# A two-layer decoder trunk on one core: the last norm's sums made on all partitions by products with ones, and its power taken on 128x256 values

## The chip, the cores and the metric

The kernel runs on one core of a Trainium2 chip. The metric is the device time of one execution in microseconds (us). The core has five engines that run side by side, each through its own instructions in order: TensorE (PE in the profile, its weight loads PEld), VectorE (DVE), ScalarE (ACT), GpSimd (POOL) and SyncE (SP), which here only issues DMA transfers. They wait for each other by semaphores. TensorE's results go into PSUM, which the kernel uses as eight banks of 128 partitions by 512 float32; the other operands lie in SBUF, as tiles of 128 partitions too.

## The reference

The reference is a trunk of two decoder layers for 256 tokens with 2048 channels. Layer 0 mixes the tokens by multi-scale retention with 8 heads, layer 1 by a short gated convolution; each is followed by a SwiGLU feed-forward of width 5632. Each sub-layer begins with an RMS norm with a scale and a shift made from a conditioning vector, its output is multiplied by a gate, and it is added to `x`. What matters here is the last step, one more RMS norm over the 2048 channels of each token with a gain for each channel:

```python
def rms_norm(x, gain=None):
    xf = x.astype(jnp.float32)
    y = xf * lax.rsqrt(jnp.mean(xf * xf, axis=-1, keepdims=True) + EPS)
    if gain is not None:
        y = y * gain.astype(jnp.float32)
    return y
...
    return rms_norm(x, final_g).astype(x.dtype)
```

## The kernel before

**Layout.** `x` lies in SBUF with channels on partitions and tokens along the row: 16 tiles `x[j]` of 128 channels by 256 tokens, in float32. A sum over the channels of a token is therefore a sum over 16 tiles and over 128 partitions.

**The bulk of the work.** The weights come from memory as blocks of 128 rows by 2048 columns (`raw`, line 290, issued by SP). Each half of a block is parted into a high part (`hi`, ScalarE, line 295) and a low part (`lo`, VectorE, line 296). For each 128 x 128 piece of weights TensorE makes three products, high with high, high with low and low with high, in `product` (lines 338 and 341) and `packed` (lines 361 to 363). The order of TensorE's instructions is that of the program (`manual_schedule`, line 188); the other engines' instructions are put in order by a scheduler with priorities.

**The last output of layer 1.** `swiglu` (line 743) ends in `output` (line 500) with `last` set. For each of the 16 column tiles, VectorE adds gate times product to `x[j]` (lines 518 and 519, for the last tile line 511, called by way of `packed` so that one instruction does). Then ScalarE squares it and VectorE adds the square to `acc` (`squares`, lines 387 and 388). The last tile's square goes into a tile of its own, `acc1` (line 512, recorded as line 384), so the norm's sum is that of two tiles, `acc = [acc, acc1]`. `with_gain` (line 792) has ScalarE multiply each new `x[j]` by the final gain into one of nine output parts (line 796).

**The last norm.** `rstd` (line 419) makes 1/sqrt(mean + eps) in three steps, each a helper that the other norms use too.

- `norm_sums` (line 391): for each half of the tokens, a product with the tile `acc` as weights and a single column of ones as the moving operand, one for each of the two tiles. Its result has one token on each partition: 128 x 2 values in PSUM (line 396).
- `norm_roots` (line 402): VectorE multiplies by 1/2048 and adds eps on 128 x 2 values (line 405); GpSimd raises them to the power -0.5 (line 407, `half` holds -0.5). What GpSimd reads and writes here lies in SBUF.
- `norm_spread` (line 410): two products, whose weights are a column of roots broadcast to 128 columns and whose moving operand is the identity matrix (line 414). Every partition then has all 256 roots in PSUM.

The result `rb` lies in PSUM. ScalarE copies it into `rbs` in SBUF (line 806). The 16 tiles of the output are multiplied by the roots, 11 of them on VectorE with `rb` from PSUM (line 810) and 5 on GpSimd with `rbs` (line 812), as `OUT_SPLIT` deals them out. When a part of one to three tiles is done, SP writes it to memory (line 813), in the order of the nine parts.

The float32 products of lines 396 and 414 leave two matmul records each in the trace; the products of the bulk leave one each.

Of the kernel before, what the change touches and what calls it, by code (L numbers as in the profile page):

```python
# [53 lines left out]


class Group:
    """Output columns of a matrix that are worked out together, in the order of their rows."""

    def __init__(self, cols, width=P, ks=range(KT)):
        self.cols, self.width, self.ks = cols, width, list(ks)  # L60


def ret_in_groups():
    """The first heads' queries, keys and gates are made of two spans of rows, the first of them ahead."""
    early, late = range(FIRST_KS), range(FIRST_KS, KT)
    ahead, heads = [], []
    for h in range(HEADS):
        q = [Q0 + h * DK + i * P for i in range(2)]
        k = [K0 + h * DK + i * P for i in range(2)]
        g = [G0 + h * DV + i * P for i in range(4)]  # L70
        v = Group([V0 + h * DV], DV)
        if h < EARLY_HEADS:
            ahead.append([q, k, g[:2], g[2:]])
            qkg = [Group(c, ks=late) for c in ahead[-1]]
        else:
            qkg = [Group(c) for c in (q, k, g[:2], g[2:])]
        heads.append((qkg, v))
    first = Group([c for pairs in ahead[:2] for pair in pairs for c in pair], ks=early)
    second = [[Group(c, ks=early) for c in pairs] for pairs in ahead[2:]]
    return first, second, heads  # L80
# [4 lines left out]


def out_groups(rows, parts, tail, lead):
    """The first columns' products with the last rows, which are made last, come after the others."""
    n = rows // P // parts
    cols = [c * P for c in range(KT)]  # L90
    out = []
    for s in range(parts):
        ks = range(s * n, (s + 1) * n)
        led = cols[:lead]
        out.append([Group(led, ks=ks[:-tail])] + [Group([c], ks=ks[-tail:]) for c in led])
        out[-1] += [Group([c], ks=ks) for c in cols[lead:]]
    return out
# [18 lines left out]


def in_use_order():
    """Each group of the weights, with its matrix and the matrix's index, in the order of use."""
    yield "ret_w_in", 0, RET_FIRST  # L120
    for groups in RET_SECOND:
        for g in groups:
            yield "ret_w_in", 0, g
    for h, (qkg, v) in enumerate(RET_HEADS):
        for g in qkg[:2] + [v] + qkg[2:]:
            yield "ret_w_in", 0, g
        if h % (HEADS // 2) == HEADS // 2 - 1:
            for g in RET_OUT[h // (HEADS // 2)]:
                yield "ret_w_out", 0, g
    for layer in range(DEPTH):  # L130
        if layer == 1:
            for g in CONV_IN:
                yield "conv_w_in", 0, g
            for g in CONV_OUT:
                yield "conv_w_out", 0, g
        for part in range(2):
            for g in FFN_IN[part]:
                yield "ffn_w_in", layer, g
            for g in FFN_OUT[part]:
                yield "ffn_w_out", layer, g  # L140


def laid_out(arrays):
    """The weights in the order of their use, as blocks of 128 rows and CHUNK columns."""
    total = sum(len(g.cols) * g.width * len(g.ks) for _, _, g in in_use_order())
    out = np.empty((total // CHUNK, P, CHUNK), np.float32)
    at = 0
    for key, i, g in in_use_order():
        for k in g.ks:
            for c in g.cols:  # L150
                o = at % CHUNK
                out[at // CHUNK, :, o : o + g.width] = arrays[key][i, k * P : (k + 1) * P, c : c + g.width]
                at += g.width
    assert at == total and total % CHUNK == 0
    return out
# [16 lines left out]
def trunk(ctx: ExitStack, tc: tile.TileContext, x_in, c_in, pos_in, w_mod, cols_in, tab_in, w_all, out):  # L172
# [14 lines left out]

    ctx.enter_context(tc.manual_schedule(engines={mybir.EngineType.PE}))

# [1 line left out]
    ones = const.tile([P, P], F32, tag="ones", name="ones")  # L191
    nc.vector.memset(ones, 1.0)
    cb = const.tile([P, D], F32, tag="cb", name="cb")
# [30 lines left out]
    half = const.tile([P, 2], F32, tag="half", name="half")  # L224
    nc.vector.memset(half, -0.5)

# [1 line left out]
    mod_a = [[const.tile([P, KT], F32, tag=f"a{l}{i}", name=f"a{l}{i}") for i in range(2)] for l in range(DEPTH)]  # L228
    mod_s = [[const.tile([P, KT], F32, tag=f"s{l}{i}", name=f"s{l}{i}") for i in range(2)] for l in range(DEPTH)]
    mod_g = [[const.tile([P, KT], F32, tag=f"g{l}{i}", name=f"g{l}{i}") for i in range(2)] for l in range(DEPTH)]  # L230
# [27 lines left out]
    units, allowed = [0], [0.0]  # L258

    def paced(n):  # L260
        """Counts n more products of 128 x 128 weights, and works out the modulations due by now."""
        units[0] += n
        due = 0
        for (a, i), (b, j) in zip(plan_mod, plan_mod[1:]):
            if units[0] >= a:
                due = min(j, i + (units[0] - a) * (j - i) // (b - a))
        allowed[0] = min(allowed[0] + n * MOST, 2.0) if n <= 64 else 0.0
        while todo and n_mod - len(todo) < due and allowed[0] >= 1.0:
            allowed[0] -= 1.0
            modulation(*todo.pop())  # L270
# [2 lines left out]
        while any(m[:2] == (layer, which) and m[2] <= last for m in todo):  # L273
            modulation(*todo.pop())

# [1 line left out]
    order = [(g, k, c) for _, _, g in in_use_order() for k in g.ks for c in g.cols]  # L277
    order.reverse()
    n_halves = w_all.shape[0] * CHUNK // HALF
# [19 lines left out]
    prepared = [0]  # L299

    def take(group, k, col):
        """The next weights' high and low parts."""
        assert order.pop() == (group, k, col)
        i = taken_cols[0] % HALF
        if i == 0:
            if ready and taken_cols[0]:
                ready.pop(0)
            while len(ready) < 1 + AHEAD * (units[0] >= early):
                n = len(ready)
                prepare()  # L310
                if len(ready) == n:
                    break
        taken_cols[0] += group.width
        return [t[:, i : i + group.width] for t in ready[0]]
# [4 lines left out]
    asides, since = [], [0]  # L319

    def ticked(n):
        """Between products, the next step of what runs beside them."""
        since[0] += n
        if asides and since[0] >= asides[0][0]:
            asides.pop(0)[1]()
            since[0] = 0

    def product(g, act, base=0, before=None, banks=None, last=True):
        """Banks [columns, (high product, the rest), tokens], one for each of the group's columns."""
        fresh = not banks  # L330
        banks = banks or [bank() for _ in g.cols]
        for k in g.ks:
# [13 lines left out]
        return banks  # L346

    def packed(g, act, base=0, before=None, between=None, banks=None):
        """Banks [columns, two of the group's columns, tokens]."""
        banks = banks or [bank() for _ in g.cols[::2]]  # L350
        for k in g.ks:
            if before:
# [20 lines left out]
        return dst  # L373

    def split(dst, src, at=slice(0, S)):
        """dst [128, (high, low), tokens] of src."""
        nc.scalar.copy(dst[:, 0, at], src)
        nc.vector.tensor_tensor(dst[:, 1, at], src, dst[:, 0, at].bitcast(F32), op=ALU.subtract)  # L378

# [1 line left out]
    def squares(acc, t, tag="acc"):  # L381
        if acc is None:
            acc = tmp(tag, bufs=1)
# [5 lines left out]
        return acc  # L389

    def norm_sums(accs):
        """The sums over partitions, a token to a partition."""
        pt = bank()
        for t in range(2):
            for i, acc in enumerate(accs):
# [4 lines left out]
        return pt  # L400

    def norm_roots(pt, n):
        """1 / sqrt(mean + eps)."""
        r = tmp("rs", (P, 2), bufs=4)
        nc.vector.tensor_scalar(r, pt[:, 0, 0:2], 1.0 / n, EPS, op0=ALU.mult, op1=ALU.add)
        r2 = tmp("rs", (P, 2), bufs=4)
# [1 line left out]
        return r2  # L408

    def norm_spread(r):  # L410
        """The roots on all partitions, in PSUM."""
        pb = bank()
        for t in range(2):
            nc.tensor.matmul(
# [27 lines left out]
    h = [h_all[:, j, :, :S] for j in range(KT)]  # L442

    def scaled_only(layer, norm, j):
        """h[j] without the norm and the shift."""
        needed(layer, SC2 if norm else SC1, j)
        a = mod_a[layer][norm][:, j : j + 1]
        nc.scalar.activation(h[j][:, 0, :], x[j], AF.Identity, scale=a)
# [2 lines left out]
        )  # L451

    def normed(accs, layer, norm, g):
        """
        The sums of the first columns, made from rows without the norm and the shift: the norm is a factor of
        each token, and the shift's product is one more token
        (twice, for these products take an even number of them). Beside them the roots, and then h, are made.
        """
        needed(layer, SH2 if norm else SH1)
        shift = mod_s[layer][norm].unsqueeze(2).to_broadcast([P, KT, 2])  # L460
        ends = [h_all[:, :, i, S:] for i in range(2)]
# [36 lines left out]
        return [lambda dst=None, pt=pt: total(pt, dst) for pt in banks]  # L498

    def output(groups, act, which, last, after=None):  # L500
        """x += gate * product; if last, tiles whose sums are those of the new x's squares."""
        layer, gate = which[0], mod_g[which[0]][which[1] == GT2]
        first, *groups = groups
        base, acc = first.ks[0], None
# [17 lines left out]
            if after:  # L522
                after(j)

# [1 line left out]
    with ExitStack() as inner:  # L526
        rm = inner.enter_context(tc.tile_pool(name="rmid", bufs=1))

# [139 lines left out]
            return both  # L668

        def mixed(head, both, v, sg):  # L670
            """The rest of a head, in steps."""
            accs, os, pts = [None], [], []

            def outputs(half):
# [27 lines left out]
            return list(zip(STEPS, [lambda: outputs(0), lambda: outputs(1), roots, ends]))  # L702

        def pair(head, i):
            """Two columns' sums [columns, two, tokens]."""
            g = RET_HEADS[head][0][i]
            (pt,) = packed(g, h)
            if (head, i) not in ahead:
# [54 lines left out]

    acc = swiglu(0, acc, lambda j: scaled_only(1, 0, j))

# [1 line left out]
    mid = [mpool.tile([P, 2, S], F32R, tag=f"mid{i}", name=name("mid")) for i in range(KT)]  # L767
    pending, done = [], 0
    for i, g in enumerate(CONV_IN):
# [29 lines left out]

    acc = swiglu(1, acc, with_gain)  # L800

# [1 line left out]
    assert not todo  # L803
    rb = rstd(acc, D)
    rbs = tmp("rbs", pool=mpool, bufs=1)
    nc.scalar.copy(rbs, rb)
    for (i, j, engine), o in zip(OUT_SPLIT, parts):
        for n in range(j - i):
            if engine == "vector":
# [39 lines left out]
```

## Time and profile before

| what | us |
|---|---|
| median of 3 runs | 2667.12 |
| lowest and highest run | 2664.53, 2668.72 |
| profiled execution, first to last instruction (its span) | 2660.6 |
| TensorE busy in it | 2621.9 (99%) |
| VectorE busy | 2017.8 (76%) |
| ScalarE busy | 1248.4 (47%) |
| GpSimd busy | 214.0 (8%) |
| mean granted TensorE clock | 0.998 of full speed |

The profile records one execution; its span is counted from its first instruction to its last, and no other time of that execution is given. The median of the runs is 6.5 us above that span. A row of a timeline gives the start in us from the span's start, the duration in us, the engine, the line of the kernel, the operation, the tiles written and read, the shapes and how many instructions were merged; in brackets the time that the engine sat idle before it, and who ended that idle time. A row on one line gives the count, the least, median and greatest duration in ns, and the first and last start in us.

### The profile page before, as it was taken

Reading aid. Unit: us, or ns where it says so; the run is one execution under the profiler, and the core shown is the slowest. Engines: PE = TensorE matmul, PEld = TensorE weight load, DVE = VectorE, ACT = ScalarE, POOL = GpSimd, SP = SyncE. Lnnn points to the kernel's source line nnn. Section 1 sums busy time; section 2 is a strip of 40 time slices with the busy share of each in tenths; the row PEclk is TensorE's granted clock in tenths of the full one; section 3 lists DMA queues with packets and bytes.
Section 4 is the critical chain, followed back from the end, with each engine's and each line's share of the span. In section 5 each row is a group of like instructions: output and inputs, shape, how many; then the busy total and the mean of one; then the engine's idle time right before and its main releaser. Section 6 shows DMA issues by size and latency. Waiting matters only on the chain.

```text
span 2660.6 us, 40134 instructions
## 1 busy us (share of the span) xinstructions
PE 2621.9 (99%) x16044; PEld 2335.6 (88%) x16044; DVE 2017.8 (76%) x2655; ACT 1248.4 (47%) x1782; POOL 214.0 (8%) x278
## 2 busy tenths in 40 slices
PE   6999999999999999999999999999999999999998
PEld 5898988999989888888888898888998888888887
DVE  8968988887698877777777889878887665555554
ACT  3444543444456444334444454444554443444443
POOL 4310000011000010100000001100000000000000
PEclk9999999999999999999999999999999999999999
DMA  9976667777677877777777768776777765555553
GB/s 374 400 265 242 251 217 296 267 270 263 250 267 261 312 281 267 298 271 284 285 268 282 268 219 321 287 282 256 268 269 256 264 220 190 185 185 189 189 190 127
DMA packets 96957, 687.69 MB, mean 258 GB/s; under 512 B 10753, under 2 KB 12545, under 8 KB 13825
## 3 DMA queue, kind: packets, MB, share of 16 engines
q1 hardware_dynamic: 96770, 685.13, 69.3%
q8 instruction: 125, 2.05, 0.3%
q14 instruction: 62, 0.51, 0.1%
HBM read 682.99 MB, written 2.10 MB: 257 GB/s over the span
## 4 chain that ended last, share of the span: by engine, by line
PE 76%; issue 19%; DVE 3%; DMA 0%; POOL 0%; ACT 0%; DVEq 0%; ACTq 0%; POOLq 0%
PE bank L338 35%; PE bank L341 18%; PE bank L363 4%; PE bank L361 4%; PE bank L362 4%; PE bank L634 2%; PE bank L635 2%; PE bank L636 2%; PE bank L477 1%; PE bank L476 1%; PE bank L478 1%; DVE raw L238 1%; DVE lo L296 1%; PE bank L680 0%; DMA raw<-w_mod 0%
## 5 line engine op out<-in xcount | busy, mean ns | idle before, releaser
L296 DVE TENSOR_TENSOR lo<-raw,hi 128x1024 fp32r<-128x1024 f32 x912 | 1113.5, 1223 | 561.1 <-ACT hi L295 559.2
L295 ACT CAST hi<-raw 128x1024 fp32r<-128x1024 f32 x912 | 953.9, 1050 | 1087.3 <-PE bank L338 638.5
L338 PE MATMUL bank<-h,hi 128*128 128x512 f32 x3296 | 1155.2, 395 | 0.0
L341 PE MATMUL bank<-h,lo 128*128 128x256 f32 x3296 | 925.5, 281 | 0.0
L338 PEld LDWEIGHTS bank<-h,hi 128*128 128x128 f32 x3296 | 622.7, 189 | 144.9
L338 PE MATMUL bank<-mid,hi 128*128 128x512 f32 x2100 | 731.1, 395 | 0.1
L341 PEld LDWEIGHTS bank<-h,lo 128*128 128x128 f32 x3296 | 623.3, 189 | 0.0
L341 PE MATMUL bank<-mid,lo 128*128 128x256 f32 x2100 | 583.8, 278 | 0.0
L338 PEld LDWEIGHTS bank<-mid,hi 128*128 128x128 f32 x2100 | 394.1, 188 | 92.2 <-DVE mid L378 0.4
L238 DVE SCALAR_TENSOR_TENSOR raw<-raw,cb 128x2048 f32<-128x2048 f32 x192 | 438.5, 2284 | 5.0 <-DMA raw<-w_mod 4.8
L341 PEld LDWEIGHTS bank<-mid,lo 128*128 128x128 f32 x2100 | 395.0, 188 | 0.0
L363 PE MATMUL bank<-h,lo 128*128 128x256 f32 x1024 | 292.4, 286 | 10.0 <-DVE lo L296 10.0
L361 PE MATMUL bank<-h,hi 128*128 128x256 f32 x1024 | 290.6, 284 | 2.8 <-ACT hi L295 2.8
L362 PE MATMUL bank<-h,hi 128*128 128x256 f32 x1024 | 290.3, 284 | 0.6 <-DVE h L432 0.5
L363 PEld LDWEIGHTS bank<-h,lo 128*128 128x128 f32 x1024 | 193.8, 189 | 14.4 <-DVE lo L296 14.4
L361 PEld LDWEIGHTS bank<-h,hi 128*128 128x128 f32 x1024 | 195.7, 191 | 3.5 <-ACT hi L295 3.3
L362 PEld LDWEIGHTS bank<-h,hi 128*128 128x128 f32 x1024 | 193.9, 189 | 2.3 <-DVE h L432 2.3
L243 POOL TENSOR_SCALAR mcol<-msum,cols 128x1 f32<-128x1 f32 x64 | 63.6, 994 | 549.6 <-DVE raw L238 549.6
L634 PE MATMUL bank<-hi,h 128*128 128x512 f32 x256 | 101.4, 396 | 0.0
L635 PE MATMUL bank<-lo,h 128*128 128x512 f32 x256 | 101.0, 395 | 0.0
L636 PE MATMUL bank<-hi,h 128*128 128x512 f32 x256 | 101.0, 394 | 0.0
L370 ACT COPY low<-bank 128x256 f32<-128x256 f32 x254 | 90.7, 364 | 11.7 <-PE bank L341 9.0
(122 smaller groups left out, 1811.6 us busy)
## 6 DMA issues: line engine op xcount, KB each, us to landing
raw<-w_all SPq DMA_DIRECT2D x456, 1024.0 KB, 4.9
raw<-w_mod SPq DMA_DIRECT2D x192, 1024.0 KB, 5.0
x<-x_in SPq DMA_DIRECT2D x4, 512.0 KB, 5.7
out<-out SPq DMA_DIRECT2D x5, 256.0 KB, 2.9
decay<-tab_in SPq DMA_DIRECT2D x8, 128.0 KB, 3.0
out<-out SPq DMA_DIRECT2D x3, 128.0 KB, 2.3
out<-out SPq DMA_DIRECT2D x1, 384.0 KB, 2.7
cols<-cols_in SPq DMA_DIRECT2D x1, 160.0 KB, 7.2
```

The costliest lines, as they stand in the source:

```text
L238: nc.vector.scalar_tensor_tensor(raw, raw, 1.0, cb, op0=ALU.mult, op1=ALU.mult, accum_out=total)
L295: nc.scalar.copy(hi, raw)
L296: nc.vector.tensor_tensor(lo, raw, hi.bitcast(F32), op=ALU.subtract)
L338: nc.tensor.matmul(pt, hi, h, start=fresh and k == g.ks[0], stop=False, skip_group_check=True)
L341: nc.tensor.matmul(pt[:, 1, :], lo, h[:, 0, :], start=False, stop=last and k == g.ks[-1], skip_group_check=True)
L361: nc.tensor.matmul(pt, hi, h[:, 0, :], start=first, stop=False, skip_group_check=True)
L362: nc.tensor.matmul(pt, hi, h[:, 1, :], start=False, stop=False, skip_group_check=True)
L363: nc.tensor.matmul(pt, lo, h[:, 0, :], start=False, stop=last, skip_group_check=True)
L370: nc.scalar.copy(low[:, at], pt[:, 1, at])
L634: nc.tensor.matmul(o, ht[:, 0, :], hi, start=k == 0, stop=False)
L635: nc.tensor.matmul(o, ht[:, 0, :], lo, start=False, stop=False)
L636: nc.tensor.matmul(o, ht[:, 1, :], hi, start=False, stop=k == KT - 1)
```

## The change

The three helpers are no longer called for the last norm; the other norms keep them. In their place:

- The whole tile of ones, 128 x 128, is the weights, and the two tiles `acc` (128 x 256) are the moving operands. The two products add up in one PSUM bank, and every partition gets the sums of all 256 tokens.
- VectorE makes the mean plus eps of 128 x 256 values, from PSUM into `mean` in SBUF.
- GpSimd takes the power of 128 x 256 values, from `mean` into `rbs` in SBUF.
- ScalarE copies `rbs` into a PSUM bank, which is the new `rb`.

The multiplications, their split between the engines and the writes stay as they are. The diff, without the comments and docstrings that it also takes out:

```diff
-    rb = rstd(acc, D)
+    pt = bank()[:, 0, :]
+    for i, t in enumerate(acc):
+        nc.tensor.matmul(pt, ones, t, start=i == 0, stop=i == len(acc) - 1)
+    mean = tmp("mean", pool=mpool, bufs=1)
+    nc.vector.tensor_scalar(mean, pt, 1.0 / D, EPS, op0=ALU.mult, op1=ALU.add)
     rbs = tmp("rbs", pool=mpool, bufs=1)
-    nc.scalar.copy(rbs, rb)
+    nc.gpsimd.tensor_tensor(rbs, mean, half[:, 0:1].to_broadcast([P, S]), op=ALU.pow)
+    rb = bank()[:, 0, :]
+    nc.scalar.copy(rb, rbs)
     for (i, j, engine), o in zip(OUT_SPLIT, parts):
```

## The prediction

> **What bounds the kernel now.** I read the page first, then the table of busy time by stage for the last 60 us, then the timeline of the last 20 us, and then the rows of single lines that price the new instructions.
>
> ```profile
> span 2660.6 us, 40134 instructions
> PE 2621.9 (99%) x16044; PEld 2335.6 (88%) x16044; DVE 2017.8 (76%) x2655; ACT 1248.4 (47%) x1782; POOL 214.0 (8%) x278
> ```
>
> ```profile
> 2600.00:2646.80 46.80, 46.80 (x292) 41.90 (x291) 24.62 (x32) 18.69 (x26) 0.00 (x0) 1.00 0.31 113
> 2646.80:2651.50 4.70, 2.33 (x14) 1.87 (x12) 0.65 (x2) 1.19 (x3) 0.69 (x1) 0.75 0.00 0
> 2651.50:2660.60 9.10, 0.00 (x0) 0.00 (x0) 3.73 (x11) 0.00 (x0) 3.46 (x5) 0.50 0.63 231
> ```
>
> The columns of the second table are the stretch and its length, the busy time and count of PE, PEld, DVE, ACT and POOL, then the granted clock, the DMA share and GB/s. The page says that TensorE bounds the kernel as a whole. That says nothing about this change, which lies behind the last weight product: up to 2646.8 TensorE is busy for 46.80 of 46.80 us, in the next 4.70 us for 2.33, and then never again. The last 14 us are a chain in which one engine at a time works and the others wait. Here is that chain:
>
> ```profile
> 2647.01 0.48 DVE L511 SCALAR_TENSOR_TENSOR x<-bank,g,x 128x256 f32<-128x256 f32 x1 [5.93 <-PE bank L363]
> 2647.52 0.42 ACT L384 ACTIVATE acc<-x 128x256 f32<-128x256 f32 x1 [6.50 <-DVE x L511]
> 2647.85 0.49 ACT L796 ACTIVATE out<-x,cols 128x256 f32<-128x256 f32 x1
> 2647.99 0.74 PEld L396 LDWEIGHTS bank<-ones,acc 128*128 128x128 f32 x6 [1.00 <-ACT acc L384]
> 2647.99 0.83 PE L396 MATMUL bank<-ones,acc 128*128 128x1 f32 x6 [0.91 <-ACT acc L384]
> 2648.86 0.16 DVE L405 TENSOR_SCALAR rs<-bank 128x2 f32<-128x2 f32 x1 [1.37 <-PE bank L396]
> 2649.10 0.69 POOL L407 TENSOR_TENSOR rs<-rs,half 128x2 f32<-128x2 f32 x1 [499.16 <-DVE rs L405]
> 2649.84 0.93 PEld L414 LDWEIGHTS bank<-tab,rs 128*128 128x128 f32 x4 [1.10 <-POOL rs L407]
> 2649.84 1.22 PE L414 MATMUL bank<-tab,rs 128*128 128x128 f32 x4 [1.02 <-POOL rs L407]
> 2651.10 0.37 ACT L806 COPY rbs<-bank 128x256 f32<-128x256 f32 x1 [2.76 <-PE bank L414]
> 2651.50 3.73 DVE L810 TENSOR_TENSOR out<-out,bank 128x256 f32<-128x256 f32 x11 [2.48 <-ACT rbs L806]
> 2651.55 3.46 POOL L812 TENSOR_TENSOR out<-out,rbs 128x256 f32<-128x256 f32 x5 [1.76 <-ACT rbs L806]
> 2652.30 5.26 SPq L813 DMA_DIRECT2D out<-out  x9
> ```
>
> Read the brackets: each instruction waited for the one above it, from the last square (2647.52 + 0.42) to the multiplications at 2651.50. Nothing else is running, so a microsecond put into this chain is a microsecond of the kernel's time, and one taken out likewise. The stretch that the change rewrites runs from 2647.99, when the last square is there, to 2651.50: **3.51 us**. That is 0.13% of the time and the most that the change can save.
>
> **The change part by part.** *Removed:* 0.87 us from 2647.99 to 2648.86 for the sums with their hand-over, then 0.24 us to GpSimd's start at 2649.10, 0.74 us to the spreading products at 2649.84, 1.26 us to the copy at 2651.10 and 0.40 us to the multiplications at 2651.50. They add up to the 3.51 us.
>
> *Added, the sums.* Two float32 products of 256 columns, each of two records. The trace has such records of 128 and of 512 columns only.
>
> ```profile
> L414 PE MATMUL bank<-tab,rs x52: 270/275/582, 21.4 to 2650.6; 128*128 128x128 f32 x52
> L199 PE MATMUL bank<-row,ones x8: 1056/1057/1187, 2.6 to 8.7; 1*128 1x512 f32 x8
> 2646.80 0.28 PE L396 MATMUL bank<-ones,acc 128*128 128x1 f32 x2
> ```
>
> On the straight line between 275 ns and 1057 ns, 256 columns take 275 + 128 x (1057 - 275) / 384 = 536 ns. The first tile's product needs only `acc`, so it runs in the gap from 2646.8 to 2647.99, where two such records (1.07 us) just fit in the 1.2 us; without that cover they would add up to 1.1 us. The last tile's two records are on the path. Bounds: 2 x 0.275 = 0.55 us if 256 columns cost no more than 128, and 2 x 1.06 = 2.1 us. I take 2 x 0.536 less a little overlap of the two, **1.0 us**, with 0.04 us of hand-over as now (2648.82 to 2648.86).
>
> *Added, the mean.* VectorE on 128x256 values from PSUM. L511 above, which also reads PSUM, took 0.48 us and two operands; a plain one with one tensor read from SBUF took 0.35:
>
> ```profile
> L534 DVE TENSOR_SCALAR acc<-acc,tab x1: 354/354/354, 106.3 to 106.3; 128x256 f32<-128x256 f32 x1
> L483 ACT COPY rb<-bank x3: 365/366/368, 816.8 to 1917.4; 128x256 f32<-128x256 f32 x3
> ```
>
> I take **0.42 us**, between the two, and 0.08 us to GpSimd's start as now (2649.02 to 2649.10).
>
> *Added, the copy into PSUM.* ScalarE has no row that writes a bank. Copies out of a bank took 0.366 us, the square from SBUF to SBUF 0.42. Bounds 0.3 to 0.5, taken **0.40 us**, with hand-overs of 0.04 and 0.03 us.
>
> *Sum without the power:* 1.0 + 0.04 + 0.42 + 0.08 + 0.04 + 0.40 + 0.03 = 2.01 us. With 3.51 us gone, the time changes by **X - 1.5 us**, where X is the duration of the power on 128x256. The bounds of the small terms move the 1.5 between 0.3 and 2.1. The multiplications behind, 11 on VectorE and 5 on GpSimd, are the same. GpSimd's may start some 0.4 us before VectorE's, as it now makes `rbs` itself, but the first write needs VectorE's first two tiles, and SP takes 5.26 us for nine writes in order, so I cost that at nothing. No other instruction is queued behind the power on GpSimd but these five, and before it the engine had been idle for 499 us.
>
> *Added, the power.* This is the whole question. These rows have prices on GpSimd:
>
> ```profile
> L407 POOL TENSOR_TENSOR rs<-rs,half x13: 688/718/3739, 20.7 to 2649.1; 128x2 f32<-128x2 f32 x13
> L245 POOL TENSOR_TENSOR a<-mcol,cols x64: 189/190/2094, 17.9 to 1717.6; 128x1 f32<-128x1 f32 x64
> L812 POOL TENSOR_TENSOR out<-out,rbs x5: 724/726/727, 2651.5 to 2654.3; 128x256 f32<-128x256 f32 x5
> 20.51 0.19 POOL L248 TENSOR_TENSOR s<-msum,cols 128x1 f32<-128x1 f32 x1 [2.24 <-DVE rs L405]
> 20.65 0.72 POOL L407 TENSOR_TENSOR rs<-rs,half 128x2 f32<-128x2 f32 x1
> ```
>
> A multiplication costs 189 ns for one element a partition and 726 ns for 256, which is 2.1 ns for each further element; a power of two elements costs 688 ns. (The maxima of 2.1 and 3.7 us fall where VectorE is at work too; in the tail VectorE waits.) So a power of two elements has 499 ns that a multiplication of one element does not have. Nothing in the trace says how much of that is paid at entry and how much for each element, because the power appears with no other size. It isn't a first use that would not come again: the first power at 20.65 took 0.72 us, right behind another instruction, the last one 0.69 us after an idle 499 us.
>
> - Upper bound: all of it per element, 249.5 ns each: X = 0.189 + 256 x 0.2495 = 64.1 us.
> - Lower bound: all of it at entry, each further element at the multiplication's 2.1 ns: X = 0.688 + 254 x 0.0021 = 1.2 us.
>
> The nearest row is the power itself, and it speaks for the upper end: two elements bring 499 ns more, where a multiplication's two bring 4. But a longer routine will also cost more to enter. As a round choice I give its entry the length of one more whole plain instruction, 189 ns; the rest is (688 - 2 x 189) / 2 = 155 ns for each element, and **X = 0.378 + 256 x 0.155 = 40 us**. The time changes by 40 - 1.5 = +38.5 us: the span from 2660.6 to 2699.1, and the median of the runs, which lies 6.5 us above the span, from 2667.1 to **2705.7 us**.
>
> [...]
>
> **The rivals.**
>
> *Overlapped elements.* GpSimd starts an element before the last is done, so the 499 ns are mostly the length of one routine and further elements come at some 25 to 75 ns. For it: the multiplication streams at 2.1 ns an element behind an entry of 189. Against it: it needs a long routine to be interleaved, and the two elements of the row already cost 499 ns. At 40 ns an element X = 0.688 + 254 x 0.040 = 10.8 us, and the time is 2667.1 + 9.3 = 2676.4 us.
>
> *Not slower: the power streams like the multiplication.* Entry 688 ns, then 2.1 ns an element: X = 1.2 us, change -0.3 us, time 2666.8 us. The place is GpSimd at its one instruction; it turns into a gain where X is below 1.5 us, and it stays within what can be told from no change (0.2%, 5.3 us) as long as X is below 6.8 us, that is (6.8 - 0.688) / 254 = 24 ns an element. For it: the row of L812. Against it: a power that needs 499 ns more for two elements would then have nearly all of its work outside its elements. Even with the sums at their lowest, the gain is under 3 us.
>
> *All of it per element.* X = 64.1 us, time 2667.1 + 62.6 = 2729.7 us. This is the far end of the forecast's own mechanism, kept in its range.
>
> *The change doesn't do what it says.* If the new chain were not alone on the path, say if the sums waited for something else, this would show as about a microsecond. TensorE's slow clock (0.75 granted in the stretch) could double the sums, +1 us. No such case reaches 0.2%.
>
> **How the numbers follow.** The forecast, paid per element with X from 20 to 64 us: 0.58. Overlapped elements, X from 6.8 to 20 us: 0.27. Streaming or nearly so, X under 6.8 us: 0.14, nearly all of it within 0.2%. Something that I have not seen that makes it faster by over 0.2%: 0.01, since only 3.51 us are there to be saved. A measurement of this kernel can tell about 0.2%, 5.3 us, from no change. So faster 0.01, same 0.14, slower 0.85. The range leaves out the streaming case below and a little at either end: from 2667.1 + 5.4 = 2672.5, just past the bound, to 2667.1 + 62.6 and 3 us of scatter between runs = 2732.5. It is wide because the cost of one instruction is known from one size only.
>
> **What would show it.** In the changed kernel's timeline, one GpSimd instruction of 128x256 behind the mean lasts about 40 us (20 to 64), and for that time every engine has nothing in it; ScalarE's copy waits for it, and then the multiplications do. The four records of the sums take about 0.5 us each, the mean 0.4 and the copy 0.4; the stretch from the last square to the first multiplication is about 42 us in place of 3.51. The weight products up to 2646.8 stay where they are. I am wrong if the power takes under 7 us; then per-element cost was misread from two elements, and the change would show only in its small terms.

## The result and the profile after

The changed kernel takes 2702.97 us (median of 4 runs, 2701.33 to 2704.76); the kernel before, run beside it, 2667.92 us (median of 4, 2664.53 to 2669.06). The ratio is 1.0134, with a 95% interval of 1.0120 to 1.0149: slower by 1.3%. A second set of runs, told below, gives 1.0155 (1.0142 to 1.0169).

The page of the changed kernel begins so:

```profile
span 2701.8 us, 40120 instructions
PE 2622.3 (97%) x16036; PEld 2334.8 (86%) x16036; DVE 2018.8 (75%) x2655; ACT 1247.0 (46%) x1782; POOL 247.9 (9%) x278
```

TensorE's busy time stands at 2622 us, as before; GpSimd's has grown from 214.0 to 247.9 us, although its number of instructions is the same 278. (Without the last norm's power that is 213.3 us before and 206.8 now, and by the sums of the groups 212 in the first experiment below and 208 in the fourth: the many small instructions differ by some us between executions, so the difference isn't read as a price.) The timeline of the end shows the new chain:

```profile
2648.86 0.60 PE L806 MATMUL bank<-acc,ones 128*128 128x256 f32 x2
2649.58 0.42 ACT L384 ACTIVATE acc<-x 128x256 f32<-128x256 f32 x1 [6.51 <-DVE x L511]
2650.05 0.70 PE L806 MATMUL bank<-acc,ones 128*128 128x256 f32 x2 [0.59 <-ACT acc L384]
2650.79 0.42 DVE L808 TENSOR_SCALAR mean<-bank 128x256 f32<-128x256 f32 x1 [1.24 <-PE bank L806]
2651.34 41.13 POOL L810 TENSOR_TENSOR rbs<-mean,half 128x256 f32<-128x256 f32 x1 [499.36 <-DVE mean L808]
2692.51 0.38 ACT L812 COPY bank<-rbs 128x256 f32<-128x256 f32 x1 [42.11 <-POOL rbs L810]
2692.55 3.47 POOL L818 TENSOR_TENSOR out<-out,rbs 128x256 f32<-128x256 f32 x5
2692.92 3.73 DVE L816 TENSOR_TENSOR out<-out,bank 128x256 f32<-128x256 f32 x11 [41.71 <-ACT bank L812]
2693.30 5.47 SPq L819 DMA_DIRECT2D out<-out  x9
```

The line to look at is the power: on 128x256 values it lasts 41.13 us. Its neighbours are as short as the instructions that they replace. By the brackets, ScalarE sat idle for 42.11 us until the power was done, and VectorE for 41.71 us until ScalarE's copy was. From the last tile's products to the first multiplication of the output it is 2692.92 - 2650.05 = 42.87 us, where it was 3.51 us: +39.36 us. The table of busy time by stage, with columns as in the prediction, shows that nothing else ran meanwhile:

```profile
2651.30:2692.50 41.20, 0.00 (x0) 0.00 (x0) 0.00 (x0) 0.00 (x0) 41.13 (x1) 0.53 0.00 0
2692.50:2701.80 9.30, 0.00 (x0) 0.00 (x0) 3.73 (x11) 0.38 (x1) 3.47 (x5) 0.50 0.61 226
```

The span grew by 2701.8 - 2660.6 = 41.2 us. Of this 39.36 us is the chain; 2.06 us is the start of the last square, 2649.58 in place of 2647.52; the rest behind the first multiplication is 0.2 us shorter (8.9 us in place of 9.1).

### The profile page after: what moved, and what is told of

Same layout as the page of the kernel before. It is cut to its first block, busy times and chain, and to the rows that moved or that the text cites. A ratio compares the mean times of both kernels' runs of the same rounds, so it can differ in the third digit from the quotient of the medians.

```text
span 2701.8 us, 40120 instructions
## 1 busy us (share of the span) xinstructions
PE 2622.3 (97%) x16036; PEld 2334.8 (86%) x16036; DVE 2018.8 (75%) x2655; ACT 1247.0 (46%) x1782; POOL 247.9 (9%) x278
## 4 chain that ended last, share of the span: by engine, by line
PE 93%; DVE 3%; POOL 2%; issue 1%; DMA 1%; ACT 0%; DVEq 0%; POOLq 0%; ACTq 0%
PE bank L338 46%; PE bank L341 23%; PE bank L363 4%; PE bank L361 4%; PE bank L362 4%; PE bank L634 2%; PE bank L635 2%; PE bank L636 2%; POOL rbs L810 2%; PE bank L477 1%; PE bank L476 1%; PE bank L478 1%; DVE raw L238 1%; DVE lo L296 1%; DMA raw<-w_mod 1%
## 5 line engine op out<-in xcount | busy, mean ns | idle before, releaser
L248 POOL TENSOR_TENSOR g<-msum,cols 128x1 f32<-128x1 f32 x64 | 35.4, 554 | 735.3 <-DVE raw L238 735.3
```

## The experiments

The theory is that of the prediction: the power on GpSimd is paid for each element along a row, and the chain at the end hides nothing. The rivals are elements overlapped in long instructions, a cost that lies in the operands' values or form, and a cost in the other parts of the change.

**Five sizes of the power.**

```diff
-    nc.gpsimd.tensor_tensor(rbs, mean, half[:, 0:1].to_broadcast([P, S]), op=ALU.pow)
+    for a, b in ((0, 8), (8, 24), (24, 56), (56, 120), (120, 256)):
+        nc.gpsimd.tensor_tensor(rbs[:, a:b], mean[:, a:b], half[:, 0:1].to_broadcast([P, b - a]), op=ALU.pow)
```

> The one power on 128x256 becomes five, on 8, 16, 32, 64 and 136 columns. Theory: each element along the row costs the same and each instruction has an entry. From the two sizes known so far, 688 ns for 2 and 41132 ns for 256, that is 159.2 ns an element and 370 ns of entry, so the five take 1.64, 2.92, 5.47, 10.56 and 22.0 us, in all 42.6 us (41.1 in one piece). Rival, elements overlapped only in long instructions or slower in them: the five don't lie on that line, the short ones nearer to the 250 ns an element that two elements would give at most (8 columns about 2.2 us).

The groups of GpSimd's instructions by line and shape, of this kernel (line, engine, operation, tiles, shapes, count, then busy us and mean ns of one):

```profile
L811 POOL TENSOR_TENSOR rbs<-mean,half 128x136 f32<-128x136 f32 x1 | 22.1, 22050 | 0.0
...
L811 POOL TENSOR_TENSOR rbs<-mean,half 128x64 f32<-128x64 f32 x1 | 10.5, 10522 | 0.0
L811 POOL TENSOR_TENSOR rbs<-mean,half 128x32 f32<-128x32 f32 x1 | 5.4, 5416 | 0.0
...
L811 POOL TENSOR_TENSOR rbs<-mean,half 128x16 f32<-128x16 f32 x1 | 2.9, 2895 | 0.0
L811 POOL TENSOR_TENSOR rbs<-mean,half 128x8 f32<-128x8 f32 x1 | 1.6, 1642 | 499.4 <-DVE mean L808 499.4
```

From 8 to 136 columns, 20408 ns for 128 elements, which is 159.4 ns an element; the entry is 1642 - 8 x 159.4 = 367 ns. By this line 16, 32 and 64 columns take 2917, 5468 and 10569 ns, within 1% of the rows, and 2 and 256 columns take 686 and 41173 ns, against 688 and 41132 in the kernel before and the changed one. All seven sizes lie on one straight line to within 1%. The five took 42.37 us from the first start to the last end, 1.24 us over the single one, as four more entries of 0.37 less some overlap. The one run took 2703.63 us, the same as the changed kernel's profiled run, but by chance: its last square started at 2648.34, 1.24 us earlier than there. The rival of overlapped elements falls: nothing gets cheaper in a long instruction.

**The power replaced by a multiplication.**

```diff
-    nc.gpsimd.tensor_tensor(rbs, mean, half[:, 0:1].to_broadcast([P, S]), op=ALU.pow)
+    nc.gpsimd.tensor_tensor(rbs, mean, half[:, 0:1].to_broadcast([P, S]), op=ALU.mult)
```

> The power is replaced by a multiplication with the same two operands, so the output is not scaled by the right roots; everything else of the change stays. Theory: the power's elements alone make the loss, so GpSimd's instruction takes about 0.73 us like the output's multiplications, the stretch from the last square to the first multiplication of the output is 2.5 us in place of 3.5 before, and the time is about 1 us under the kernel before (ratio 0.9996, nothing that can be told from 1). Rival, the broadcast operand or something else of the change costs: GpSimd's instruction stays at several us, or the time stays above that of the kernel before.

The timeline of this kernel:

```profile
2648.24 0.70 PE L806 MATMUL bank<-acc,ones 128*128 128x256 f32 x2 [0.59 <-ACT acc L384]
2648.98 0.42 DVE L808 TENSOR_SCALAR mean<-bank 128x256 f32<-128x256 f32 x1 [1.24 <-PE bank L806]
2649.54 0.61 POOL L810 TENSOR_TENSOR rbs<-mean,half 128x256 f32<-128x256 f32 x1 [499.03 <-DVE mean L808]
2650.18 0.38 ACT L812 COPY bank<-rbs 128x256 f32<-128x256 f32 x1 [1.59 <-POOL rbs L810]
...
2650.59 3.73 DVE L816 TENSOR_TENSOR out<-out,bank 128x256 f32<-128x256 f32 x11 [1.19 <-ACT bank L812]
```

With the same operands, the same broadcast and the same number of elements, GpSimd takes 0.61 us in place of 41.13. From the last tile's products to the first multiplication it is 2650.59 - 2648.24 = 2.35 us, 1.16 us less than in the kernel before. The median is 2663.88 us (11 runs) beside 2667.04 us (15 runs), ratio 0.9991 (0.9982 to 1.0000). So the loss is the power's, and the other parts of the change are worth about 1 us, too little to be told apart in the runs' times.

**The power of ones.**

```diff
-    nc.gpsimd.tensor_tensor(rbs, mean, half[:, 0:1].to_broadcast([P, S]), op=ALU.pow)
+    nc.gpsimd.tensor_tensor(rbs, ones[:, 0:1].to_broadcast([P, S]), half[:, 0:1].to_broadcast([P, S]), op=ALU.pow)
```

> The power is taken of ones, read from one broadcast column, in place of the means, so the output is not scaled by the right roots. Theory: the routine takes the same time whatever the values, 41.1 us. Rival: the cost depends on the values, and 1.0, whose power is 1.0, takes a shorter way, well under 30 us.

The rows of that line, then GpSimd's timeline around it and the row of the last square, and who waited:

```profile
L810 POOL TENSOR_TENSOR rbs<-ones,half x1: 41236/41236/41236, 807.0 to 807.0; 128x256 f32<-128x256 f32 x1
```

```profile
806.97 41.24 POOL L810 TENSOR_TENSOR rbs<-ones,half 128x256 f32<-128x256 f32 x1 [2.88 <-PE bank L363]
848.17 0.19 POOL L248 TENSOR_TENSOR g<-msum,cols 128x1 f32<-128x1 f32 x1
848.32 0.69 POOL L407 TENSOR_TENSOR rs<-rs,half 128x2 f32<-128x2 f32 x1
...
2682.34 0.42 ACT L384 ACTIVATE acc<-x 128x256 f32<-128x256 f32 x1 [6.24 <-DVE x L511]
```

```profile
PEld bank L414 <- POOL rs L407: 32.9, 1, 32.9
```

The power of 1.0 takes 41.24 us, so these two inputs give no sign that the values matter. The run also showed what I had not planned. As the power no longer depends on the sums, the scheduler issued it at 807 us, in the middle of the bulk. There GpSimd's order put it ahead of the power of another norm (line 407, at 848.32; in the kernel before at 812.17). TensorE's spreading product waited 32.9 us for that. The run took 2691.75 us: the 41 us had moved from the end to the middle, and a large part was paid there. The last square started at 2682.34, 34.8 us later than in the kernel before. Behind it there were 7.7 us in place of 13.1, as the output's multiplications no longer waited for the sums, so the time of this run alone doesn't price the power. The power itself took 0.1 us longer than at the end.

**Half of the partitions.**

```diff
-    nc.gpsimd.tensor_tensor(rbs, mean, half[:, 0:1].to_broadcast([P, S]), op=ALU.pow)
+    for a, b, op in ((0, 64, ALU.pow), (64, P, ALU.mult)):
+        nc.gpsimd.tensor_tensor(rbs[a:b], mean[a:b], half[a:b, 0:1].to_broadcast([b - a, S]), op=op)
```

> The power is taken on partitions 0 to 63 alone, 64x256 values; the other 64 partitions are multiplied in its place, so half of the output's channels are not scaled by the right roots. Theory: the cost goes by the elements along a row and not by the partitions, so the power takes 41.1 us as on 128 partitions, and the multiplication adds about 0.7. Rival: it goes by the number of values, and takes 20.6 us.

The rows of that line, least, median and greatest of the two instructions:

```profile
L811 POOL TENSOR_TENSOR rbs<-mean,half x2: 612/20870/41127, 2656.0 to 2697.2; 64x256 f32<-64x256 f32 x2
```

The power on 64 partitions takes 41127 ns, on 128 it took 41132. (The median of two is a mean and tells nothing.) Half of the partitions cost as much as all of them; the elements along the row are what is paid. The one run took 2708.89 us.

**The root on ScalarE and VectorE.**

```diff
+    eps = const.tile([P, 1], F32, tag="eps", name="eps")
+    nc.vector.memset(eps, EPS)
...
-    mean = tmp("mean", pool=mpool, bufs=1)
-    nc.vector.tensor_scalar(mean, pt, 1.0 / D, EPS, op0=ALU.mult, op1=ALU.add)
-    rbs = tmp("rbs", pool=mpool, bufs=1)
-    nc.gpsimd.tensor_tensor(rbs, mean, half[:, 0:1].to_broadcast([P, S]), op=ALU.pow)
+    std = tmp("mean", pool=mpool, bufs=1)
+    nc.scalar.activation(std, pt, AF.Sqrt, scale=1.0 / D, bias=eps)
     rb = bank()[:, 0, :]
-    nc.scalar.copy(rb, rbs)
+    nc.vector.reciprocal(rb, std)
+    rbs = tmp("rbs", pool=mpool, bufs=1)
+    nc.scalar.copy(rbs, rb)
```

> GpSimd's power is gone: ScalarE takes the square root of the sums on all partitions straight from PSUM (scale 1/2048, bias eps), VectorE makes the reciprocal of 128x256 values into a PSUM bank and goes on to the output, and ScalarE copies it for GpSimd. Theory: the sums on all partitions are worth having as soon as the power isn't taken on GpSimd; the stretch from the last square to the first multiplication is about 0.74 + 0.04 + 0.42 + 0.04 + 0.42 = 1.7 us in place of 3.56 before and 42.9 in the changed kernel, so the time is about 2 us under the kernel before, which is under what can be told from no change (ratio 0.999). Rival: the new operations bring costs of their own, a table load of 1.28 us on ScalarE that waits with the root, or a reciprocal of some us, and the stretch is no shorter than before.

The timeline of this kernel:

```profile
2649.13 0.70 PE L808 MATMUL bank<-acc,ones 128*128 128x256 f32 x2 [0.59 <-ACT acc L386]
2649.49 1.28 ACT L810 ACT_TABLE_LOAD   x1
2650.79 0.47 ACT L810 ACTIVATE mean<-bank,eps 128x256 f32<-128x256 f32 x1
2651.30 1.76 DVE L812 RECIPROCAL bank<-mean 128x256 f32<-128x256 f32 x1 [2.67 <-ACT mean L810]
2653.09 0.37 ACT L814 COPY rbs<-bank 128x256 f32<-128x256 f32 x1 [1.83 <-DVE bank L812]
2653.49 3.73 DVE L818 TENSOR_TENSOR out<-out,bank 128x256 f32<-128x256 f32 x11 [0.44 <-ACT rbs L814]
```

The 41 us are gone, but here the rival was right: behind the table load of 1.28 us the root starts 0.96 us after the sums have ended, and the reciprocal takes 1.76 us. From the last tile's products to the first multiplication it is 4.36 us, 0.85 us more than in the kernel before. The median is 2665.25 us (12 runs) beside 2664.66 us (16 runs), ratio 1.0003 (0.9995 to 1.0012): no difference that can be told. No kernel of this study that computes the whole reference beats the one before; what is left to be gained in these 3.5 us lies below what the runs' times resolve.

**The changed kernel once more.** No edit.

> The changed kernel once more, unedited, with more executions of both kernels. The chain at the end is 39.4 us longer in the two profiled executions, the medians of the first few runs are 35 us apart. Theory: the difference is scatter of the bulk between executions, so the profile's stretch is again 42.9 us, and the medians are between 35 and 40 us apart. Rival: the change makes the bulk in front of the last norm some 4 us shorter, and the last square starts 4 us earlier than in the kernel before in execution after execution.

In the timeline of this profiled run the last square is later, not earlier, and the power is as long:

```profile
2651.89 0.42 ACT L384 ACTIVATE acc<-x 128x256 f32<-128x256 f32 x1 [6.51 <-DVE x L511]
...
2653.65 41.13 POOL L810 TENSOR_TENSOR rbs<-mean,half 128x256 f32<-128x256 f32 x1 [499.24 <-DVE mean L808]
```

The medians are 2707.35 us (4 runs) and 2664.66 us (16 runs), 42.7 us apart, where I had expected 35 to 40. The ratio of 1.0155 (1.0142 to 1.0169) means 38 to 45 us; the first comparison's interval means 32 to 40 us. The 39.4 us of the chain lie in both. I read the first 35 us as a low draw and these 42.7 as a high one. Over all runs the medians are 2704.9 us (8 runs of the changed kernel) and 2666.1 us (35 of the kernel before), 38.8 us apart. The rival, a last square that starts some 4 us earlier, is not borne out: it starts at 2649.58 and 2651.89 in the two profiles of the changed kernel, at 2647.52 in the one of the kernel before. In the other experiments that leave the power or its replacement at the end it starts between 2647.78 and 2654.2. So the bulk scatters by some us between executions; where that comes from was not looked into.

## Why the prediction was right

**What bounds the stretch** held: every added microsecond of the power appeared in the chain, and the table by stage shows all other engines at 0.00 for 41.20 us. The sign that the weight products end where they did, at 2646.8, did not come: TensorE turned to the sums at 2648.86 and 2651.16 in the two profiles, by the scatter of the bulk.

**The power.** Forecast 40 us, measured 41.13. The mechanism, paid for each element, is shown by the five sizes. The size was luck as much as reading: from the single size in the trace only 1.2 to 64 us could be had, and that the entry of 378 ns and 155 ns an element came so near to 367 and 159.4 rests on a round choice, the entry taken as two plain instructions. That the power costs more to enter than a multiplication, an assumption then, came out so: 367 ns, where the multiplication's 189 ns for one element leave 187 without the element's 2.1, an estimate. What the routine does for one element no run shows. The reading that did the work was to set 688 ns for two powers beside 189 ns for one multiplication, and to ask what the other 499 ns would do with 256 elements.

**The other terms.** Without the power I had 2.01 us; measured 42.87 - 41.13 = 1.74 us. The term that was mis-sized is the sums: I had 1.0 us, and they took 0.70. A record of 256 columns lasted 0.38 us, or 0.48, not the 0.54 of my line between 128 and 512 columns:

```profile
L806 PE MATMUL bank<-acc,ones x4: 378/380/483, 2648.9 to 2650.4; 128*128 128x256 f32 x4
```

The line's far end, 1057 ns for 512 columns, was taken from the first microseconds of the kernel and was no good guide; why it wasn't, no run shows. The slow clock that I feared for the sums did not come: from 2650.00 to 2650.80 the granted clock was 1.00. In the kernel before it was 0.50 from 2649.84 to 2651.06, and the four spreading records there took 421 to 582 ns, where the median of all 52 is 275; but the four from 21.4 us on took as long, 422 to 582 ns, at a clock of 1.00, so what the clock alone does to a record no run shows. The mean took 0.42 us as forecast, the copy 0.38 against 0.40. The sum is X - 1.77 us in place of X - 1.5.

**The time.** 2705.7 us forecast, 2702.97 measured. I set the chain's change on the median of the runs, and that was right; the 6.5 us that I took as lying around the span were not all of that kind. The profiled run of the changed kernel took 2703.63 us with a span of 2701.8, so 1.8 us lie around it. The profile of before had caught one of the faster executions: 2660.6 + 1.8 = 2662.4 us, an estimate, where the 35 runs go from 2662.10 to 2672.57 us. That the forecast came within 2.7 us is partly luck, as the two comparisons of the same kernels gave 35.1 and 42.7 us. Two sums end a little off, and nothing hangs on them: 2667.1 + 38.5 is 2705.6, and the range's upper end, 2729.7 + 3, is 2732.7.

**The rivals.** Overlapped elements (2676.4 us) and streaming (2666.8 us) both fell by the five sizes. Streaming is what the multiplication does: 613 ns for 256 elements in the power's place. With 189 ns for one element that is (613 - 189) / 255 = 1.7 ns for each further element, and the output's multiplications come to (726 - 189) / 255 = 2.1 ns, both estimates. The rate does not hold for the power: its 159.4 ns are about 76 times the 2.1, an estimate too. Half of the partitions cost as much as all of them, 41127 ns beside 41132; how the engine deals its work out to the partitions no run shows.

## What to carry to other kernels

Price an instruction by the work that it does for each element along the row, not by its engine's rate for simple operations: two elements of a costly operation, set beside one element of a cheap one, give bounds for 256, though far apart (1.2 and 64 us here); a second size of the costly operation itself gives the price. Costly elementwise work belongs on as few columns as it can be spread to, with all 128 partitions filled: here 128x2 with two spreading products costs 2 us, and 128x256 without them costs 41. And an instruction of 41 us isn't hidden just because its engine is busy 8% of the time: the power of ones at 807 us stood ahead of a short power that TensorE needed, and TensorE waited 32.9 us.

## What the runs showed that I had not expected

The power's cost is a straight line over seven sizes, 367 ns + 159.4 ns an element, to within 1%. The reciprocal on VectorE took 1.76 us for 128x256 where the means of its instructions with that output size in the kernel before are 0.28 to 0.48 us. The copies of the roots and VectorE's first multiplication, which both read the same PSUM bank, ran one behind the other (copy 2653.09 to 2653.46, multiplication at 2653.49, "0.44 <-ACT rbs"), also in the kernel before (2651.10 to 2651.47, then 2651.50); whether they have to was not tried.
